# First attention of a two-layer encoder: where the values of the last four heads are projected among the filler work

## The chip, the cores and the metric

The kernel runs on one core of one Trainium2 chip. The metric is device time in microseconds (us) of one execution; lower is better. Engines are named as in the profile: PE (TensorE, matrix products), PEld (its weight loads), DVE (VectorE), ACT (ScalarE), POOL (GpSimd) and SP (SyncE, which here only issues DMAs).

## The reference

A sequence of 512 positions with 1024 features passes two layers. The first is multi-head latent attention with 8 heads and a feed-forward block, the second chunked attention on shared keys and values with a feed-forward block. The change touches only the first attention. Cut to that, it computes:

```python
a = h @ w_a
cq, ckv, kr = split(a, [384, 384 + 256])
q  = (rms_norm(cq, g_q) @ w_uq)          # 8 heads x (128 + 64 rotary)
kv = (rms_norm(ckv, g_kv) @ w_ukv)       # 8 heads x (128 keys + 128 values)
s  = (q_nope . k_nope + q_rope . k_rope) * scale, masked by chunks of 64
o  = softmax(s) @ v
y  = o @ w_o
```

Inputs and output are float32.

## The kernel before, in words

**Numbers as pairs.** A float32 operand of a product is split in a high part (a cast on ACT, L144) and the rest (a subtraction on DVE, L145). A product is then three matmuls (`mm3`, L355 to L358): high by high, low by high, high by low. So each weight chunk and each result that is multiplied again costs one ACT and one DVE instruction. In the profile the weight parts are called `whi` and `wlo`.

**Weights.** `feed` holds a list of weight chunks in the order of their use (L724 to L753). A chunk is loaded by SP into one of five `raw` buffers, split into one of three pairs `whi`, `wlo`, and used. `feed.next` hands out the next chunk and the list must be in the order in which the work asks; `feed.ahead` splits one chunk in advance. The 1024-column chunk `w_uv[1]` holds the value weights of heads 4 to 7, a 640-column chunk `w_qk[h]` the query and key weights of head h, `w_uqr[0]` and `w_uqr[1]` the rotary query weights.

**PSUM.** Results of matmuls go to eight banks (`bank`, L92): four with the tag "mm" for all projections and the products with the values, two "s" for scores, two "t" for transposes. A tile keeps its bank until ACT and DVE have read it.

**First attention.** `attention` (L513) walks through 8 heads x 4 blocks of 128 queries. At each step it computes the scores of a block, transposes the probabilities of an earlier one, and at every fourth step does a head's product with the values (`pv`, L1013). Between these it weaves in units of filler work, so that PE has something to do while softmax runs on DVE and ACT. The filler is the generator `fill_a` (L986): values of heads 0 to 3 (`values_a(0)`, four tiles of 128 positions, 8 units), the norm of the queries, the rotary queries of heads 0 to 3 (`rotary(0)`), the rotary key, head 0's queries and keys (`heads_a(0)`, 6 units), and so on. `start_a(0)` runs the filler up to head 0; `attention` then takes 13 units before the first scores (the argument `first` at L1038), and from there about 1.6 units a step. `until` takes as many units as are needed to reach a mark: head h's mark before its scores, the mark "v" before a product with the values.

**Names.** `values_a(c)` (L888) writes a values tile `b` into `va0` to `va3`; its split is brought forward by 90 places of priority where c is 1 (L899). `heads_a(h)` (L924) makes `qh`, `ql` (high and low part of the queries) and `kh`, `kl` (keys), each a buffer of the 15 of tag "a", which also hold the four rotary query tiles `qr` of a half. `rotary` (L902) makes `ra`, `rb`, `rh`, `rl` and copies parts of them into `qr` by 16 small DMAs. `rotary_key` (L977) makes `kr1` and `kr2`. `query_norm` (L971) makes `nsq`, with one power on POOL (L452). `cqh`, `cql` and `ckh`, `ckl` are the low-rank queries and keys that all these projections read.

The order on each engine is set at build time by a scheduler, by the order of the code and the priorities (`first(n)`); on the chip each engine runs its own list strictly in that order and waits on semaphores for the others.

Of the kernel before, what the change touches and what calls it, by code (L numbers as in the profile page):

```python
# [21 lines left out]
H_A, NOPE, ROPE, VD = 8, 128, 64, 128  # L22
# [46 lines left out]
def trunk(ctx: ExitStack, tc: tile.TileContext, a, out):  # L69
# [16 lines left out]
    def U(dt=F32, name="u"):  # L86
        return up.tile([P, S], dt, tag="u", name=name_(name), bufs=NU)
# [4 lines left out]
    def bank(tag="mm", name="b"):  # L92
        return ps.tile([P, S], F32, tag=tag, name=name_(name), bufs={"mm": 4, "s": 2, "t": 2}[tag])

    def small(name="sm"):
        return sp.tile([P, 4], F32, tag="small", name=name_(name))
# [38 lines left out]
    @contextmanager  # L135
    def first(n):

        tc.cur_priority -= n
        yield
        tc.cur_priority += n  # L140


    def split(dst_hi, dst_lo, src):
        return (nc.scalar.copy(dst_hi, src),  # L144
                V.tensor_tensor(dst_lo, src, dst_hi.bitcast(F32), op=OP.subtract))  # L145
# [203 lines left out]
    feed = Feed()  # L349
# [5 lines left out]
    def mm3(o, l, r, start, stop):  # L355
        nc.tensor.matmul(o, l[0], r[0], start=start, stop=False)  # L356
        nc.tensor.matmul(o, l[0], r[1], start=False, stop=False)  # L357
        nc.tensor.matmul(o, l[1], r[0], start=False, stop=stop)  # L358
# [24 lines left out]
    def cut(t, c):  # L383
        return t[0][:, c], t[1][:, c]
# [80 lines left out]
    def spread(col, first=0):  # L465

        b = bank("t", "bc")
        for i in range(col.shape[1]):
            nc.tensor.transpose(b[:, (first + i) * P:(first + i + 1) * P],
                                col[:, i:i + 1].to_broadcast([P, P]), ident)  # L470
        return b
# [255 lines left out]
        feed.add(a["w_aq"][k], 768)  # L727
    feed.add(a["w_uv"][0], 1024)
    feed.add(a["w_uqr"][0], 768)
    feed.add(a["w_qk"][0], 640)  # L730
    feed.add(a["w_uv"][1], 1024)
    for h in range(1, H_A):
        if h == 4:
            feed.add(a["w_uqr"][1], 768)
        feed.add(a["w_qk"][h], 640)
# [50 lines left out]
    for k in range(KT):  # L786
        h, l = U(F32R, "xh"), U(F32R, "xl")
# [68 lines left out]
    for j in range(2):  # L856
        V.tensor_tensor(ckv[j], ckv[j], rkv, op=OP.mult)
        h, l = U(F32R, "ckh"), U(F32R, "ckl")
# [9 lines left out]
    for j in range(3):  # L868
        h, l = U(F32R, "cqh"), U(F32R, "cql")
# [9 lines left out]
    def A(name):  # L879
        return pool[0].tile([P, S], F32R, tag="a", name=name_(name), bufs=15)  # L880
# [7 lines left out]
    def values_a(c):  # L888

        w = feed.next(1024, False)  # L890
        for tt in range(NQT):
            if tt == 1:
                feed.ahead()
            b = bank()
            ts_ = slice(tt * P, (tt + 1) * P)
            for k in range(2):
                mm3(b, cut(cks[k], ts_), w(k * S, S), k == 0, k == 1)
                yield True
            with first(90 if c else 0):  # L899
                split(va[tt][:, 0, c * S:(c + 1) * S], va[tt][:, 1, c * S:(c + 1) * S], b)  # L900

    def rotary(half):  # L902

        b = [bank() if half else bank("s") for _ in range(2)]
        yield from proj(2, 3, 3, cqs, b, False)
        pc = []
        for (m1, m2, op) in ((cos, sin, OP.subtract), (sin, cos, OP.add)):
            ta, tb = U(name="ra"), U(name="rb")
            V.tensor_tensor(ta, b[0], m1, op=OP.mult)
            V.tensor_tensor(tb, b[1], m2, op=OP.mult)  # L910
            V.tensor_tensor(ta, ta, tb, op=op)
            h, l = U(F32R, "rh"), U(F32R, "rl")
            split(h, l, ta)
            pc.append((h, l))
        for hh in range(4):
            q = A("qr")
            for part in range(2):
                for i in range(2):
                    d = (part * 2 + i) * 32
                    nc.sync.dma_start(q[d:d + 32].bitcast(F32),  # L920
                                      pc[i][part][hh * 32:(hh + 1) * 32].bitcast(F32))
            qr[4 * half + hh] = q

    def heads_a(h):  # L924
        bq = bank()
        w = feed.next(640, False)
        for k in range(3):
            if k == 2:
                feed.ahead()
            mm3(bq, w(k * P, P), cqs[k], k == 0, k == 2)  # L930
            yield True
        qh, ql, kh, kl = (A(n) for n in ("qh", "ql", "kh", "kl"))
        split(qh, ql, bq)
        bk = bank()
        for k in range(2):
            mm3(bk, w((3 + k) * P, P), cks[k], k == 0, k == 1)
            yield True
        split(kh, kl, bk)
        qk_a[h] = qh, ql, kh, kl
        yield h  # L940

    def out_first(rhs):


        late = []
        for i in range(2):
            while i and not fill.scored:
                yield False
            b = [bank("s" if i else "mm") for _ in range(2)]
            firsts.extend(b)  # L950
            for c in range(2):
                w = feed.next(1024, False)
                for k in range(4 * c, 4 * c + 4):
                    if k == 4 * c + 1:
                        feed.ahead()

                    def step(k=k, b=b, w=w):
                        while len(rhs) <= k:
                            yield False
                        for j in range(2):  # L960
                            mm3(b[j], w(k % 4 * 256 + j * P, P), rhs[k], k == 0, k == KT - 1)
                            yield True

                    if k < KT - 1:
                        yield from step()
                    else:
                        late.append(step())
        for t in late:
            yield from t

    def query_norm():  # L971
        for j in range(3):
            sq_.add(b2[j])
        rq = rstd_of_scaled(sq_.total(), QL, r0)
        V.tensor_scalar(nsq, rq, -((NOPE + ROPE) ** -0.5), None, op0=OP.mult)

    def rotary_key():  # L977

        nc.gpsimd.tensor_tensor(sik[:64], kr[64:], sik[64:], op=OP.mult)
        nc.gpsimd.tensor_tensor(kr[:64], kr[:64], cos[:64], op=OP.mult)  # L980
        nc.gpsimd.tensor_tensor(kr[:64], kr[:64], sik[:64], op=OP.add)
        for e in (LO, HI):
            nc.scalar.copy(kr1[e], kr[:64])
            V.tensor_tensor(kr2[e], kr[:64], kr1[:64].bitcast(F32), op=OP.subtract)

    def fill_a():  # L986
        yield from values_a(0)
        query_norm()
        yield from rotary(0)
        rotary_key()  # L990
        yield from heads_a(0)
        yield from values_a(1)
        yield "v"
        for h in range(1, H_A):
            if h == 4:
                yield from rotary(1)
            yield from heads_a(h)
        yield from out_first(osp)

    def start_a(h):  # L1000
        fill.until(h)
        qh, ql, kh, kl = qk_a.pop(h)
        r = qr.pop(h)

        def qk(o, qt, n):
            q_ = slice(qt * P, (qt + 1) * P)
            nc.tensor.matmul(o, qh[:, q_], kh[:, :n], start=True, stop=False)
            nc.tensor.matmul(o, qh[:, q_], kl[:, :n], start=False, stop=False)
            nc.tensor.matmul(o, ql[:, q_], kh[:, :n], start=False, stop=False)
            nc.tensor.matmul(o, r[:, q_], kr1[:, :n], start=False, stop=False)  # L1010
            nc.tensor.matmul(o, r[:, q_], kr2[:, :n], start=False, stop=True)

        def pv(pth, ptl):  # L1013
            fill.until("v")
            o = bank()
            v_ = slice(h * VD, (h + 1) * VD)
            for kt in range(NQT):
                q_ = slice(kt * P, S)
                mm3(o[:, q_], (va[kt][:, 0, v_], va[kt][:, 1, v_]), (pth[:, kt, q_], ptl[:, kt, q_]),
                    kt == 0, kt == NQT - 1)  # L1020
            V.reciprocal(sums, sums)
            of = U(name="of")
            nc.scalar.copy(of, o)

            def rest():
                V.tensor_tensor(of, of, spread(sums), op=OP.mult)
                oh, ol = U(F32R, "oh"), U(F32R, "ol")
                split(oh, ol, of)
                osp.append((oh, ol))

            return rest

        sums = small("sums")
        return Head(qk, lambda n: mask[:, S - n:], lambda qt: nsq[:, qt:qt + 1], pv, sums)

    firsts = []
    fill = Filler(fill_a())
    attention(H_A, start_a, fill, 13, 8 + 5 * 7 + 6 + 14, False)  # L1038
    fill.drain()
# [592 lines left out]
    fill = Filler(fill_b())  # L1632
# [108 lines left out]
```

## Time and profile before

| | |
|---|---|
| median of 3 timed runs | 1124.07 us (1122.27 to 1124.4) |
| profiled execution, own time | 1122.24 us |
| its span, first to last instruction | 1120.5 us |
| instructions | 18982 |
| mean granted clock of PE | 0.998 |

Tables of the profile give the busy time of an engine and its share of the span. A row of the timeline has the start in us from the span's start, the duration, the engine, the line of the kernel, the operation, the tile that is written and those that are read, their shapes, and the number of merged instructions; in brackets stands the idle time before it and what ended that. Instructions on PE overlap, so the step from one start to the next says more than a duration. A row of the waits names who waited for whom, the total in us, how many times, and the longest.

### The profile page before, as it was taken

The numbers are of one execution on the slowest core, as the hardware profiler recorded it, in microseconds if no ns is written. First come the engines' busy times: TensorE is split into PE (matmuls) and PEld (weight loads), VectorE is DVE, ScalarE is ACT, GpSimd is POOL, SyncE is SP. The second block draws the span as 40 slices with busy tenths as digits, with TensorE's granted clock in tenths as the row PEclk, the third lists the DMA queues.
The fourth block names the chain that finished last, engine by engine and source line by source line (L and its number), as shares of the span: only waits on it lengthen the run. The fifth ranks groups of instructions, "written<-read, shape, count | busy, mean of one in ns | idle before, by whom it ended". The sixth has DMA issues, their size and how long they took to land.

```text
span 1120.5 us, 18982 instructions
## 1 busy us (share of the span) xinstructions
PE 1104.6 (99%) x6973; PEld 984.4 (88%) x6973; DVE 932.4 (83%) x1671; ACT 685.5 (61%) x1339; POOL 69.1 (6%) x106
## 2 busy tenths in 40 slices
PE   9999999999999999999999999999999999999997
PEld 6788889999999998887788888889999999998885
DVE  6787737999989889978868887758999899889977
ACT  6476636755555556768435767656755555566675
POOL 1200000000000001400000000000000000002402
PEclk9999999999999999999999999999999999999999
DMA  7342216323232358861556565635423322459923
GB/s 234 107 117 67 85 56 227 133 70 107 94 127 95 125 167 241 145 202 29 193 150 168 142 178 148 165 103 181 148 78 95 125 84 95 142 169 289 172 57 76
DMA packets 62990, 150.85 MB, mean 135 GB/s; under 512 B 8432, under 2 KB 10224, under 8 KB 62896
## 3 DMA queue, kind: packets, MB, share of 16 engines
q1 hardware_dynamic: 55552, 136.61, 38.7%
q0 software_dynamic: 6912, 12.59, 6.8%
q8 instruction: 55, 0.90, 0.3%
q10 hardware_dynamic: 432, 0.44, 0.1%
q14 instruction: 39, 0.32, 0.1%
HBM read 119.52 MB, written 9.63 MB: 115 GB/s over the span
## 4 chain that ended last, share of the span: by engine, by line
PE 46%; DVE 3%; DMA 2%; issue 1%; ACT 1%; POOL 0%; SPq 0%; POOLq 0%; DVEq 0%; ACTq 0%
PE al L1446 8%; PE b L356 6%; PE b L357 6%; PE b L358 6%; PE be L1446 4%; PE al L1197 4%; PE be L1197 3%; PE ga L1446 2%; PE pt L508 1%; PE de L1197 1%; PE ga L1197 1%; PE b L1600 1%; PE b L1599 1%; PE sc L1592 1%; PE sc L1591 1%
## 5 line engine op out<-in xcount | busy, mean ns | idle before, releaser
L144 ACT CAST whi<-raw 128x1024 fp32r<-128x1024 f32 (+3 forms) x224 | 225.5, 1007 | 212.6 <-PE al L1446 73.0
L145 DVE TENSOR_TENSOR wlo<-raw,whi 128x1024 fp32r<-128x1024 f32 (+3 forms) x224 | 261.3, 1168 | 57.7 <-ACT whi L144 54.3
L1446 PE MATMUL al<-th,whi 128*128 128x256 f32 x432 | 123.0, 285 | 0.4 <-DVE ut L1458 0.3
L1446 PE MATMUL al<-th,wlo 128*128 128x256 f32 x432 | 121.2, 281 | 0.0
L1446 PE MATMUL al<-tl,whi 128*128 128x256 f32 x432 | 121.0, 280 | 0.0
L356 PE MATMUL b<-xh,whi 128*128 128x512 f32 (+1 forms) x304 | 117.6, 387 | 0.1
L357 PE MATMUL b<-xl,whi 128*128 128x512 f32 (+1 forms) x304 | 113.0, 372 | 0.1
L358 PE MATMUL b<-xh,wlo 128*128 128x512 f32 (+1 forms) x304 | 112.4, 370 | 0.3 <-DVE wlo L145 0.3
L174 DVE TENSOR_TENSOR raw<-raw,raw 128x1024 f32<-128x1024 f32 x72 | 86.7, 1220 | 1.2 <-DMA raw<-in_w_pair 0.9
L1446 PEld LDWEIGHTS al<-th,whi 128*128 128x128 f32 x432 | 81.3, 188 | 2.9 <-DVE ut L1458 0.8
L1446 PEld LDWEIGHTS al<-th,wlo 128*128 128x128 f32 x432 | 81.3, 188 | 0.4 <-DVE wlo L145 0.4
L1446 PEld LDWEIGHTS al<-tl,whi 128*128 128x128 f32 x432 | 81.3, 188 | 0.0
L496 ACT ACTIVATE p<-p,mn 128x128 f32<-128x128 f32 (+1 forms) x96 | 54.0, 563 | 39.5 <-DVE mn L494 38.4
L145 DVE TENSOR_TENSOR ptl<-pt,pth 128x128 fp32r<-128x128 f32 (+1 forms) x96 | 46.7, 487 | 29.4 <-ACT pth L144 23.7
L358 PEld LDWEIGHTS b<-xh,wlo 128*128 128x128 f32 x304 | 57.5, 189 | 10.1 <-DVE wlo L145 0.7
L144 ACT CAST whi<-wd 128x512 fp32r<-128x512 f32 x86 | 49.9, 620 | 26.8 <-PE al L1197 11.9
L145 DVE TENSOR_TENSOR wlo<-wd,whi 128x512 fp32r<-128x512 f32 x86 | 56.5, 689 | 11.5 <-ACT whi L144 11.2
L356 PEld LDWEIGHTS b<-xh,whi 128*128 128x128 f32 x304 | 57.7, 190 | 7.5 <-ACT xh L148 1.0
L357 PEld LDWEIGHTS b<-xl,whi 128*128 128x128 f32 x304 | 57.7, 190 | 7.3 <-DVE xl L149 1.4
L144 ACT CAST pth<-pt 128x128 fp32r<-128x128 f32 (+1 forms) x96 | 40.4, 421 | 26.6 <-PE pt L508 25.6
L1197 PE MATMUL al<-whi,ph 128*128 128x512 f32 x132 | 51.9, 393 | 0.5 <-ACT y L1258 0.5
L1197 PE MATMUL al<-whi,pl 128*128 128x512 f32 x132 | 51.5, 391 | 0.0
(309 smaller groups left out, 3267.4 us busy)
## 6 DMA issues: line engine op xcount, KB each, us to landing
raw<-in_w_pair SPq DMA_DIRECT2D x72, 512.0 KB, 3.6
wd<-in_w_down SPq DMA_DIRECT2D x54, 256.0 KB, 5.6
raw<-in_w_o SPq DMA_DIRECT2D x16, 512.0 KB, 3.5
raw<-in_w_gu SPq DMA_DIRECT2D x16, 512.0 KB, 3.8
raw<-in_w_down SPq DMA_DIRECT2D x16, 512.0 KB, 4.1
raw<-in_w_qkb SPq DMA_DIRECT2D x16, 512.0 KB, 3.5
wd<-in_w_down POOLq DMA_DIRECT2D x22, 256.0 KB, 5.6
wd<-raw POOLq DMA_DIRECT2D x22, 256.0 KB, 4.2
```

Of the source, the lines that this page charges most:

```text
L144: return (nc.scalar.copy(dst_hi, src), V.tensor_tensor(dst_lo, src, dst_hi.bitcast(F32), op=OP.subtract))
L145: V.tensor_tensor(dst_lo, src, dst_hi.bitcast(F32), op=OP.subtract))
L174: V.tensor_tensor(t, x, y, op=OP.add)
L356: nc.tensor.matmul(o, l[0], r[0], start=start, stop=False)
L357: nc.tensor.matmul(o, l[0], r[1], start=False, stop=False)
L358: nc.tensor.matmul(o, l[1], r[0], start=False, stop=stop)
L496: nc.scalar.activation(p[:, :n], p[:, :n], AF.Exp, bias=mn[:, :1], scale=-1.0, accum_out=self.sums[:, qt:qt + 1])
L508: nc.tensor.transpose(t[:, kt * P:(kt + 1) * P], p[:, kt * P:(kt + 1) * P], ident)
L1197: nc.tensor.matmul(to[e], l[c], r[d], start=j < 4 and k == 0 and n == 0, stop=k == NF // 2 - 1 and n == 2, skip_group_check=True)
L1446: nc.tensor.matmul(o, l[c], r[d], start=first_ and n == 0, stop=k == K2 - 1 and n == 2, skip_group_check=True)
L1591: nc.tensor.matmul(o, q1[:, e, q_], k1[:, e, :n], start=True, stop=False)
L1592: nc.tensor.matmul(o, q1[:, e, q_], k2[:, e, :n], start=False, stop=True)
```

## The change: the second half of the values goes behind head 2

The values of heads 4 to 7 (`values_a(1)`) and their mark "v" move in the filler from behind head 0's queries and keys to behind head 2's; the weight list is reordered to match; and only heads 4 to 7 ask for the mark before their product with the values.

```diff
     feed.add(a["w_uv"][0], 1024)
     feed.add(a["w_uqr"][0], 768)
-    feed.add(a["w_qk"][0], 640)
-    feed.add(a["w_uv"][1], 1024)
-    for h in range(1, H_A):
+    for h in range(H_A):
+        if h == 3:
+            feed.add(a["w_uv"][1], 1024)
         if h == 4:
             feed.add(a["w_uqr"][1], 768)
         feed.add(a["w_qk"][h], 640)
...
         rotary_key()
-        yield from heads_a(0)
-        yield from values_a(1)
-        yield "v"
-        for h in range(1, H_A):
+        for h in range(H_A):
+            if h == 3:
+                yield from values_a(1)
+                yield "v"
             if h == 4:
                 yield from rotary(1)
             yield from heads_a(h)
...
         def pv(pth, ptl):
-            fill.until("v")
+            if h >= 4:
+                fill.until("v")
```

No instruction is added or taken away. What the scheduler makes of it is seen in the engines' lists. Each row has the line, the operation, the tile written and the tiles read, the shape, and in brackets the engines that it waits for.

First PE, in the 13 units ahead of the first scores. Before, behind the second values tile of the second half (`b_166`) the third one (`b_167`) begins:

```order
L356 MATMUL b_166_735<-whi_154_697,ckh_102_465 128x512
L357 MATMUL b_166_735<-wlo_155_698,ckh_102_465 128x512
L358 MATMUL b_166_735<-whi_154_697,ckl_103_466 128x512
L356 MATMUL b_167_744<-whi_154_697,ckh_100_460 128x512 [waits DVE_49]
L357 MATMUL b_167_744<-wlo_155_698,ckh_100_460 128x512
```

Now, at that place, head 1's keys (`b_170`) end, head 0's first score matmul follows (`sc_181`), and head 2's queries (`b_171`) begin:

```order
L357 MATMUL b_170_742<-ckl_103_466,whi_154_697 128x512
L358 MATMUL b_170_742<-ckh_102_465,wlo_155_698 128x512
L1007 MATMUL sc_181_786<-kh_158_706,qh_156_704 128x128 [waits DVE_49,Activation_49]
L356 MATMUL b_171_751<-cqh_111_525,whi_164_729 128x512 [waits DVE_49]
L357 MATMUL b_171_751<-cql_112_526,whi_164_729 128x512
```

The four values tiles stand behind head 2's keys now, in between the scores of head 0; from the end of the fourth on PE's list is as it was.

Second DVE, while PE is there. Before:

```order
L462 TENSOR_TENSOR r2_134_614<-r_133_612,r_81_356 128x4 [waits Pool_49]
L145 TENSOR_TENSOR rl_143_649<-ra_140_643,rh_142_648 128x512 [waits Activation_49]
L975 TENSOR_SCALAR nsq_537<-r2_134_614 128x4 [waits DVE_49]
L145 TENSOR_TENSOR va0_543<-b_162_720,va0_543 128x512 [waits Activation_49]
L909 TENSOR_TENSOR ra_144_652<-b_135_617,sin_91_406 128x512
L910 TENSOR_TENSOR rb_145_653<-b_136_618,cos_92_407 128x512
L145 TENSOR_TENSOR va1_544<-b_166_735,va1_544 128x512 [waits Activation_49]
L911 TENSOR_TENSOR ra_144_652<-ra_144_652,rb_145_653 128x512 [waits DVE_49]
L145 TENSOR_TENSOR va2_545<-b_167_744,va2_545 128x512 [waits Activation_49]
L145 TENSOR_TENSOR rl_147_658<-ra_144_652,rh_146_657 128x512 [waits Activation_49]
L145 TENSOR_TENSOR ql_157_705<-b_152_688,qh_156_704 128x512 [waits Activation_49]
```

Now (`wlo_174` is the low part of the moved value weights, `wlo_186` that of head 3's query and key weights):

```order
L145 TENSOR_TENSOR wlo_174_761<-raw_153_695,whi_173_760 128x1024 [waits PE_49,Activation_49]
L145 TENSOR_TENSOR rl_143_649<-ra_140_643,rh_142_648 128x512 [waits Activation_49]
L909 TENSOR_TENSOR ra_144_652<-b_135_617,sin_91_406 128x512
L910 TENSOR_TENSOR rb_145_653<-b_136_618,cos_92_407 128x512
L145 TENSOR_TENSOR wlo_186_804<-raw_163_727,whi_185_803 128x640 [waits DMAHW6_49,PE_49,Activation_49]
L911 TENSOR_TENSOR ra_144_652<-ra_144_652,rb_145_653 128x512 [waits DVE_49]
L145 TENSOR_TENSOR rl_147_658<-ra_144_652,rh_146_657 128x512 [waits Activation_49]
L984 TENSOR_TENSOR kr2_118_539<-kr_104_469,kr1_117_538 64x512 [waits Activation_49]
L984 TENSOR_TENSOR kr2_118_539<-kr_104_469,kr1_117_538 64x512
L145 TENSOR_TENSOR ql_157_705<-b_152_688,qh_156_704 128x512 [waits Activation_49]
L145 TENSOR_TENSOR kl_159_707<-b_160_710,kh_158_706 128x512 [waits Activation_49]
```

The three `va` rows that emptied values tiles are gone from among the rotary rows, and weight splits of 1024 and 640 columns and the two `kr2` stand ahead of `ql_157`, which empties head 0's query tile `b_152`.

Third ACT, at the same time. Before:

```order
L144 CAST whi_171_771<-raw_153_695 128x640 [waits DVE_49,DMAHW3_49,PE_49,Activation_49]
L144 CAST rh_142_648<-ra_140_643 128x512 [waits DVE_49]
L144 CAST va0_543<-b_162_720 128x512 [waits PE_49]
L144 CAST va1_544<-b_166_735 128x512 [waits PE_49]
L144 CAST va2_545<-b_167_744 128x512 [waits PE_49]
L144 CAST rh_146_657<-ra_144_652 128x512 [waits DVE_49]
L144 CAST qh_156_704<-b_152_688 128x512
```

Now:

```order
L144 CAST whi_173_760<-raw_153_695 128x1024 [waits DVE_49,DMAHW3_49,PE_49,Activation_49]
L144 CAST rh_142_648<-ra_140_643 128x512 [waits DVE_49]
L144 CAST whi_185_803<-raw_163_727 128x640 [waits DMAHW6_49,PE_49,Activation_49]
L144 CAST rh_146_657<-ra_144_652 128x512 [waits DVE_49]
L983 CAST kr1_117_538<-kr_104_469 64x512 [waits Pool_49]
L983 CAST kr1_117_538<-kr_104_469 64x512
L144 CAST qh_156_704<-b_152_688 128x512
```

The casts of the values tiles are gone from here, and a weight cast and the two halves of the rotary key stand ahead of `qh_156`.

## The prediction

> **What bounds the kernel now.** I read the page's busy times first, then stretches of the window in which the change lies, then the waits of TensorE (PE) there, then the instructions themselves.
>
> ```profile
> PE 1104.6 (99%) x6973; PEld 984.4 (88%) x6973; DVE 932.4 (83%) x1671; ACT 685.5 (61%) x1339; POOL 69.1 (6%) x106
> ```
>
> PE is busy for 99% of the span, so time that PE loses is lost for good unless a later wait of PE shrinks by as much. By the two orders of instructions, PE's rows 230 to 306 are rearranged and every other row of PE is the same; VectorE (DVE) differs in its rows 77 to 124 and ScalarE (ACT) in 55 to 86. In the trace of before PE's rows 230 to 306 run from 56.68 to 73.37 us.
>
> ```profile
> 56.70:60.00 3.30, 3.18 (x14) 2.35 (x13) 2.73 (x8) 2.24 (x4) 1.02 (x1) 1.00 0.47 130
> 60.00:63.40 3.40, 3.27 (x14) 2.36 (x13) 3.38 (x7) 2.11 (x5) 0.00 (x0) 1.00 0.46 107
> 63.40:66.80 3.40, 3.40 (x17) 2.80 (x16) 3.31 (x7) 3.37 (x7) 0.00 (x0) 1.00 0.41 96
> ```
>
> The columns are the stretch, its length, then busy us of PE, PEld, DVE, ACT and POOL, and the granted clock. PE hardly idles here, and DVE is as full as PE from 60 to 66.8. So nothing is to be gained on PE but 0.12 + 0.13 us and what the overlap hides; and DVE has no room for being asked earlier. Where PE does wait:
>
> ```profile
> 56.68 0.39 PE L356 MATMUL b<-whi,ckh 128*128 128x512 f32 x1
> 59.17 0.39 PE L358 MATMUL b<-whi,ckl 128*128 128x512 f32 x1
> 59.69 0.50 PE L356 MATMUL b<-whi,ckh 128*128 128x512 f32 x1
> 60.95 0.40 PE L358 MATMUL b<-whi,ckl 128*128 128x512 f32 x1
> 61.48 0.50 PE L356 MATMUL b<-whi,ckh 128*128 128x512 f32 x1
> PEld b L356 <- DVE va L145: 1.1, 2, 0.6
> ```
>
> Between the first two rows lie eleven steps of 0.227 us (2.49 / 11), the pace of 512-column matmuls. Behind 59.17 and behind 60.95 a step takes 0.52 and 0.53, each time at the first matmul of a values tile. The third and fourth values tile wait until DVE's `va` has emptied the PSUM bank of the first and second: four banks serve all projections (tag "mm"), and the two others hold head 0's queries and keys, which ACT and DVE have not got to. That is the key to the change: **banks, emptied by two engines in a fixed order**.
>
> **The change, step by step.** In the new order, head 1's queries and keys stand where two and a half values tiles stood. Each head's tiles keep their banks until `ql` and `kl` are written; a values tile is emptied early, by its raised priority. So at head 2's first matmul (PE row 246) the four banks hold head 0's q and k and head 1's q and k, and none is emptied. Which comes free first, and when? DVE's row 96 (`ql` of head 0). I follow DVE there from lengths of before.
>
> ```profile
> 52.92 1.22 DVE L145 TENSOR_TENSOR wlo<-raw,whi 128x1024 fp32r<-128x1024 f32 x1
> 55.32 0.82 DVE L145 TENSOR_TENSOR wlo<-raw,whi 128x640 fp32r<-128x640 f32 x1
> 56.73 0.17 DVE L448 TENSOR_SCALAR v<-v 128x4 f32<-128x4 f32 x1
> 56.97 1.02 POOL L452 TENSOR_TENSOR r<-v,mhalf 128x4 f32<-128x4 f32 x1 [9.16 <-DVE v L448]
> 56.70 0.73 ACT L144 CAST whi<-raw 128x640 fp32r<-128x640 f32 x1 [3.16 <-PE b L357]
> 49.87 1.08 ACT L144 CAST whi<-raw 128x1024 fp32r<-128x1024 f32 x1
> ```
>
> DVE's row 77 now splits 640 weight columns in place of 1024, 0.40 less, so `v` comes at 56.33, POOL's power ends at about 57.6 and `r`, `nsq` are written by 57.9. The 1024-column split has moved into row 87. Its ACT half can't start before 56.70, when PE has read the buffer it goes into, and ends at 57.78. So DVE starts row 87 at 57.9.
>
> ```profile
> 59.55 0.68 DVE L909 TENSOR_TENSOR ra<-b,sin 128x512 f32<-128x512 f32 x1
> 60.15 0.68 DVE L910 TENSOR_TENSOR rb<-b,cos 128x512 f32<-128x512 f32 x1
> 62.06 0.62 ACT L144 CAST rh<-ra 128x512 fp32r<-128x512 f32 x1
> 63.65 1.26 ACT L983 CAST kr<-kr 64x512 fp32r<-64x512 f32 x2
> 64.52 1.38 DVE L984 TENSOR_TENSOR kr<-kr,kr 64x512 fp32r<-64x512 f32 x2
> ```
>
> Starts on DVE are 0.60 apart for 512 columns, 0.74 for 640 and 1.13 for 1024. Row 87: 57.92 to 59.05. `rl`, `ra`, `rb`: to 60.85. `wlo` of head 3's weights, which stands ahead now: to 61.59 (its ACT half waits for PE's last read of head 1's weights, near 60.0, and is done by 60.8). `ra`: ends at 62.27. ACT's `rh` then takes 62.31 to 62.93, DVE's `rl` 62.96 to 63.56, the two `kr2` 1.38, to 64.94; ACT has written `qh` by 64.7. So `ql` runs from 64.94 to **65.6**, and head 2's matmul starts at 65.7. PE gets there after 15 matmuls of 0.227 from 56.68 and one short score matmul, at 60.1.
>
> **Term 1: a new wait of 5.5 us.** Its ends: 5.0 (ten steps read to 0.05 each) and 6.6 (POOL's power has a row twice as long):
>
> ```profile
> 28.52 2.07 POOL L452 TENSOR_TENSOR r<-v,mhalf 128x4 f32<-128x4 f32 x1 [13.98 <-DVE v L448]
> ```
>
> Behind the waiting matmul stands all of PE, the scores of head 0 too, and with them DVE's and ACT's softmax. Nothing covers it: PE runs in order, and the values matmuls (24 of 0.227, 5.4 us) that filled just this time are behind it now.
>
> **Term 2: minus 0.6.** The two waits of before (0.52 and 0.53 less 0.23 each) go, as values tiles meet banks that DVE empties at 66.2 (`kl`), 66.8 and 67.4, before PE asks.
>
> **Term 3: plus 0.4.** The emptying of four values tiles and of head 2's keys now falls among head 0's softmax. Head 2's `kl` takes the first buffer of the 15 that carry these operands, and waits for head 0's last score; behind it on DVE wait `va`, head 0's last mask step and the exponent on ACT, and at the end the last `ptl`, which the first product with the values reads.
>
> ```profile
> 71.76 0.40 PE L356 MATMUL b<-ckh,whi 128*128 128x512 f32 x1
> 72.61 0.74 DVE L494 CUSTOM_DVE_ANT_0 p<-sc,mask,nsq 128x512 f32<-128x512 f32 x1
> 74.01 0.72 ACT L496 ACTIVATE p<-p,mn 128x512 f32<-128x512 f32 x1
> 76.80 0.69 DVE L145 TENSOR_TENSOR ptl<-pt,pth 128x512 fp32r<-128x512 f32 x1
> 78.48 0.39 PE L357 MATMUL b<-ptl,va 128*128 128x512 f32 x1
> ```
>
> PE's stream asks for `ptl` 6.72 after head 0's scores (78.48 - 71.76); before, it was there at 77.49, 1.0 early. Now: 0.3 for the last score, 0.60 `kl`, 0.60 `va`, 0.67 mask, 1.0 exponent with its sum, then ACT's values copy, weight split, two exponents and three `pth`, and DVE's last 640 columns and `ptl`: about 7.1, so 0.4 late (0 to 0.8).
>
> **Term 4: the clock.** The trace has one long pause of PE, its end, and one long cold stretch, its start.
>
> ```profile
> 1112.65:1116.07 3.42, 0.47 (x3) 0.05 (x1) 2.51 (x6) 0.72 (x2) 1.00 (x1) 1.00 0.21 77
> 1116.07:1119.48 3.41, 0.00 (x0) 0.00 (x0) 1.39 (x3) 0.00 (x0) 0.00 (x0) 0.50 0.64 231
> 1.19 4.02 PE L113 MATMUL warm<-idle 128*128 128x512 bf16 x9 [1.19 <-DVE idle L110]
> 6.10 0.78 PE L357 MATMUL b<-xl,whi 128*128 128x512 f32 x1
> 6.69 0.42 PE L358 MATMUL b<-xh,wlo 128*128 128x512 f32 x1
> 6.95 0.40 PE L356 MATMUL b<-xh,whi 128*128 128x512 f32 x1
> ```
>
> After 0.47 us of work in the 3.42 us up to 1116.07 the clock falls to 0.50, 2.95 us after the last work ended (1112.65 + 0.47). At the start a 512-column matmul takes 0.45 (4.02 over nine), twice the 0.23 of later, and the short step returns at 6.7, 5.5 us after PE's first work. The new pause has one 128-column matmul in 5.5 us, near its end, when `kh` is there (65.1), and behind the last one's end (60.25) 4.8 us of nothing. That is longer than 2.95, so the clock likely falls. Then PE runs at half speed for between 3.0 us (as short as the fall took) and 5.5 (as at the start), and half of that is lost: 1.5 to 2.8. Without a fall the price is nothing. I take 1.75, nearer to the short end, as the start's 5.5 had waits for its operands in it.
>
> The Trainium skill, "TensorE: Matmul & The Clock Gate", section "What's actually happening", says that PE falls to half its clock after an idle window of about 3.4 us and comes back after a busy one, and that the windows run freely, whatever the kernel does. By that page one window at half speed would cost an estimated 1.7 us, and a pause of 5.5 us can also end with no whole idle window in it. The trace agrees on the fall: 0.47 us of work in 3.42 was little enough.
>
> **What costs nothing.** The values' weights are asked for one place later in SP's queue:
>
> ```profile
> 37.95 0.35 SPq L287 DMA_DIRECT2D raw<-in_w_qk  x1
> raw<-in_w_uv SPq DMA_DIRECT2D x2, 512.0 KB, 5.0
> qr<-rl SPq DMA_DIRECT2D x16, 64.0 KB, 2.0
> ```
>
> The issue near 38 now carries 512 KB, landing at 43; ACT reads it at 56.7. The 16 small rotary copies keep their count and shift by under 1 us; head 0's last is issued near 64 and there by 66.5, while PE reads it at about 69.8. If these covers went, each would add its delay to the same wait.
>
> **Sum.** 5.5 - 0.6 + 0.4 + 1.75 = 7.05 us. The profiled execution took 1122.24 us (span 1120.5 and 1.74 around it), so 1129.3 on its scale. The three timed runs have a median of 1124.07, 1.8 above it, which would give 1131.1. I predict between them, **1130.2 us**.
>
> **Rivals.**
> - *The clock stays up.* For it: the pause is only about 2 us longer than the time the clock took to fall, and a matmul stands in it. Against: no shorter pause is shown that kept it. Time: 1122.24 + 5.3 = 1127.5 (1129.4 by the median).
> - *The bank is free in time* (the other side). The wait for `ql` decides: if DVE wrote head 0's `ql` by 60.1, no pause would come, and only the two old waits would go, 1122.24 - 0.6 = 1121.6, no change. For it: head 0's queries are complete at 55.3, and only order keeps `ql` back. Against: DVE has 7.0 us of work and waits in line from 57.9 on, ACT's `rh` among it. The time is level with `ql` at 60.7, and 0.2% longer with `ql` at 63.
> - *The delay is taken up later.* PE's waits after 80 us, ten kinds, come to 5.3 us:
>
> ```profile
> PE b L357 <- DVE wlo L149: 1.3, 1, 1.3
> ...
> PE b L356 <- DVE ra L909: 0.2, 1, 0.2
> ```
>
>  If all of them were for work that doesn't follow PE, 7.05 - 5.3 = 1.75 would be left: 1124.0. Against: each is for DVE, ACT or POOL working on what PE made just before, and so shifts with PE.
>
> **How the numbers follow.** Forecast with the clock's fall 0.80; clock stays 0.14; taken up later 0.03; bank in time 0.03. The range runs from the second case's low end (1122.24 + 5.0 - 0.6 + 0 = 1126.6, drawn in to 1127.0) to the forecast's high end by the median (1124.07 + 6.6 - 0.6 + 0.8 + 2.8 = 1133.7): 1127.0 to 1133.5. Slower by over 0.2% (2.2 us, about what a measurement of this kernel can tell from no change) is 0.94, within it 0.05, faster 0.01.
>
> **What would show it.** In the profile after: PE idle of about 5.5 us from 60.1 to 65.7, ended by DVE's `ql`, L145; a stretch of granted clock 0.50 behind it and steps of 0.45 there; no wait of PE at the values tiles; a short wait for `ptl` at head 0's first product with the values; from there on the same stream as before, about 7 us later. I am wrong if PE waits for under 3 us there, if `ql` is written long before 65, or if the shift at 80 us isn't that at the end.

## The result, and the profile after

| | before | after |
|---|---|---|
| median, 4 timed runs each | 1123.17 us (1120.22 to 1124.4) | 1128.85 us (1128.65 to 1130.33) |
| ratio | | 1.0064 [1.0051, 1.0078] |
| profiled execution, own time | 1122.24 us | 1130.33 us |
| mean granted clock of PE | 0.998 | 0.995 |

The kernel became slower. The ratio 1.0064 means 0.64% of 1123.17 = 7.2 us (5.7 to 8.8 by the interval). It isn't the quotient of the two medians of four, which lie 5.7 us apart, at the low end of the interval. On another chip (e5 below) the medians lie 7.4 us apart. The figure predicted was 1130.2, in a range from 1127.0 to 1133.5.

The page's line of busy times, after:

```profile
PE 1107.8 (98%) x6973; PEld 987.2 (87%) x6973; DVE 933.2 (83%) x1671; ACT 685.3 (61%) x1339; POOL 69.0 (6%) x106
```

PE has as many instructions as before and is busy 3.2 us longer (1107.8 against 1104.6): the same work ran slower somewhere. The rest of the loss must be idle time. The two longest waits of PE after, then the waits of its weight loads (PEld) between 54 and 90 us:

```profile
PE sc L1007 <- ACT kh L144: 5.0, 1, 5.0
PE b L357 <- DVE wlo L149: 1.3, 1, 1.3
...
PEld sc L1007 <- ACT kh L144: 5.4, 1, 5.4
PEld b L356 <- DVE ql L145: 0.2, 1, 0.2
```

The wait of 1.3 was there before; the one of 5.0 is new, and the two at values tiles (1.1 together) are gone. The profile puts the new pause down to head 0's first score, which lacks `kh`. The very next matmul, head 2's first, then lacks a bank until DVE's `ql`, but only 0.2 of its wait is left to show. When two matmuls in a row have to wait, the first one's wait covers most of the second's, so the instruction behind a long wait is worth a look as well. PE's timeline has them one behind the other.

```profile
56.74 0.39 PE L356 MATMUL b<-cqh,whi 128*128 128x512 f32 x1
59.92 0.39 PE L358 MATMUL b<-ckh,wlo 128*128 128x512 f32 x1
65.30 0.47 PE L1007 MATMUL sc<-kh,qh 128*128 128x128 f32 x1 [4.99 <-ACT kh L144]
65.79 0.79 PE L356 MATMUL b<-cqh,whi 128*128 128x512 f32 x1
66.81 0.63 PE L358 MATMUL b<-cqh,wlo 128*128 128x512 f32 x1
67.23 0.63 PE L356 MATMUL b<-cqh,whi 128*128 128x512 f32 x1
71.45 0.40 PE L356 MATMUL b<-whi,ckh 128*128 128x512 f32 x1
```

The first row is PE's first rearranged one, at 56.74 (56.68 before); the second is the last of head 1's 15 matmuls. At their pace the next would start at 59.92 + 0.23 = 60.15. One score matmul of 0.06 between them makes 60.21 for head 2's first, which starts at 65.79: 5.6 us. The step from 66.81 to 67.23 is 0.42 where it was 0.23. Head 2's 15 matmuls take 71.45 - 65.79 = 5.66 us in place of 15 x 0.227 = 3.41: another 2.25.

DVE's timeline shows what the bank waited for, and one row of ACT what the score waited for:

```profile
57.98 1.23 DVE L145 TENSOR_TENSOR wlo<-raw,whi 128x1024 fp32r<-128x1024 f32 x1
61.66 0.69 DVE L911 TENSOR_TENSOR ra<-ra,rb 128x512 f32<-128x512 f32 x1
63.03 0.69 DVE L145 TENSOR_TENSOR rl<-ra,rh 128x512 fp32r<-128x512 f32 x1 [0.68 <-ACT rh L144]
63.64 1.38 DVE L984 TENSOR_TENSOR kr<-kr,kr 64x512 fp32r<-64x512 f32 x2
65.04 0.69 DVE L145 TENSOR_TENSOR ql<-b,qh 128x512 fp32r<-128x512 f32 x1
64.65 0.59 ACT L144 CAST kh<-b 128x512 fp32r<-128x512 f32 x1
```

DVE works without a gap from 57.98, waits once for ACT's `rh`, and ends `ql` at 65.04 + 0.69 = 65.73; PE goes on at 65.79. ACT is hardly earlier: it writes `qh`, which `ql` reads, from 64.17 to 64.76 and `kh` from 64.65 to 65.24. So head 0's tiles stand late in the lists of both engines. Stretches of after, with the columns as before (length, busy us of PE, PEld, DVE, ACT, POOL, then the granted clock), cut where the clock changes:

```profile
60.12:63.54 3.42, 0.18 (x1) 0.00 (x0) 2.74 (x5) 1.86 (x3) 0.00 (x0) 1.00 0.41 96
63.54:66.95 3.41, 1.63 (x4) 1.25 (x5) 3.37 (x7) 2.67 (x5) 0.00 (x0) 0.50 0.37 87
66.95:70.36 3.41, 3.41 (x10) 2.64 (x9) 0.58 (x1) 0.33 (x1) 0.00 (x0) 0.50 0.46 106
70.36:73.77 3.41, 3.41 (x19) 2.84 (x18) 1.92 (x4) 2.55 (x4) 0.00 (x0) 1.00 0.59 192
```

The clock is at half from 63.54 to 70.36, 6.82 us, with PE at work on the projections in the last 4.57 of them. Half of 4.57 is 2.3, which is the 2.25 just read from the matmuls.

So the loss has two parts in one place, a pause and the cold stretch behind it. The experiments ask whether the banks are its cause, what holds `ql` back, and whether the clock's share is real.

### The profile page after: what moved, and what is told of

Same layout as the page of the kernel before. It is cut to its first block, busy times and chain, and to the rows that moved or that the text cites. A ratio compares the mean times of both kernels' runs of the same rounds, so it can differ in the third digit from the quotient of the medians.

```text
span 1128.5 us, 18984 instructions
## 1 busy us (share of the span) xinstructions
PE 1107.8 (98%) x6973; PEld 987.2 (87%) x6973; DVE 933.2 (83%) x1671; ACT 685.3 (61%) x1339; POOL 69.0 (6%) x106
## 4 chain that ended last, share of the span: by engine, by line
PE 45%; DVE 4%; DMA 2%; issue 1%; ACT 1%; POOL 0%; SPq 0%; POOLq 0%; DVEq 0%; ACTq 0%
PE al L1447 8%; PE b L356 5%; PE b L357 5%; PE b L358 5%; PE be L1447 4%; PE al L1198 4%; PE be L1198 3%; PE ga L1447 2%; PE de L1198 1%; PE ga L1198 1%; PE pt L508 1%; PE b L1601 1%; PE b L1600 1%; PE sc L1593 1%; DVE wlo L145 1%
```

## The experiments

The first four ran on one chip, where before took 1121.2 us (median of 20 runs, 1119.72 to 1123.95), the last four on another, where it took 1120.03 (21 runs, 1118.83 to 1121.67). Ratios are against these.

### e1_own_buffers: the rotary tiles get buffers of their own

The theory says that head 0's `ql` is late because it stands late in DVE's list (and `qh` in ACT's), and that it stands there because `qh`, `ql`, `kh`, `kl` share 15 buffers with the four rotary query tiles `qr`, handed out in the order of the code. Here the same 15 buffers are divided, 4 and 11.

```diff
-        return pool[0].tile([P, S], F32R, tag="a", name=name_(name), bufs=15)
+        if name == "qr":
+            return pool[0].tile([P, S], F32R, tag="qr", name=name_(name), bufs=4)
+        return pool[0].tile([P, S], F32R, tag="a", name=name_(name), bufs=11)
```

> The changed kernel, with the four rotary query tiles in buffers of their own (4) and the heads' operands in the 11 others, so that head 0's ql need not be ordered behind the rotary copies; in DVE's list ql of head 0 moves from row 96 to row 85. Bank theory (PE pauses because head 0's q and k hold their PSUM banks until DVE and ACT reach them behind the rotary work): ql is written before 59 us, no wait of PE over 1 us between 56 and 75 us, granted clock 1.00 throughout, ratio to before 0.998 to 1.002. Rival (the scores of head 0 wait for the rotary work itself, and the banks are only what the wait looks like): PE still idles 4 to 5 us somewhere before 68 us, ratio 1.004 to 1.007.

Measured: 1120.73 us, ratio 0.9994 [0.9984, 1.0005]. The loss is gone. DVE's row, PE's only wait between 54 and 90 us, and two stretches:

```profile
55.55 0.68 DVE L145 TENSOR_TENSOR ql<-b,qh 128x512 fp32r<-128x512 f32 x1
...
PE sc L1009 <- DVE mn L494: 0.3, 1, 0.3
...
60.00:63.40 3.40, 3.40 (x18) 2.81 (x16) 3.40 (x7) 3.03 (x6) 0.00 (x0) 1.00 0.47 109
63.40:66.80 3.40, 3.40 (x22) 2.98 (x21) 3.35 (x6) 2.49 (x5) 0.00 (x0) 1.00 0.37 87
```

`ql` now starts 9.5 us earlier (55.55 against 65.04; of that 0.9 is this execution's earlier start, with head 1's first matmul at 55.83 against 56.74), and ACT's `qh` moves by as much, from 64.17 to 54.67. PE is busy for all of 60 to 66.8, and the clock stays at 1.00. The values are still behind head 2. So the place of the values costs nothing by itself; **the order in which the banks come free is the cause, and the shared buffers set that order**. How the scheduler gets from shared buffers to such an order is read from the code; no run shows it. One thing moved with it: head 0's first score now stands behind head 2's matmuls, so this run removes the wait for `kh` along with that for the bank. Which of the two would hold PE without the other is the question of e4.

### e2_dummies: PE kept at work in the pause

Twenty more matmuls, whose result nobody reads, stand behind head 1's keys, 20 x 0.227 = 4.5 us in the pause of after. They add work that the reference doesn't have. If the clock's share is real, it goes while the wait stays.

```diff
+            if h == 2:
+                o = bank("t", "dummy")
+                for _ in range(20):
+                    nc.tensor.matmul(o, cks[0][0][:, :P], cks[0][0], start=True, stop=True)
```

> The changed kernel with 20 matmuls of 512 columns added behind head 1's keys, whose result nobody reads: they fill 4.5 of the 5.4 us in which PE idles and change no wait. Clock theory (2.1 us of the loss are matmuls at half clock behind the pause): the first matmul of head 2 stands at 65.8 us as in the changed kernel, the steps behind it are 0.23 and not 0.43, the granted clock is 1.00 from 60 to 75 us, and the kernel is 2.1 us shorter than the changed one: ratio to before 1.004 to 1.005. Rival (the clock costs nothing, since DVE and ACT set the pace there): same time as the changed kernel, ratio 1.0064.

Measured: 1126.75 us, ratio 1.0048 [1.0033, 1.0063], granted clock 0.998 to 0.999 in every run. PE's timeline and two stretches:

```profile
59.22 4.70 PE L995 MATMUL dummy<-ckh 128*128 128x512 f32 x20
64.39 0.33 PE L1011 MATMUL sc<-kh,qh 128*128 128x128 f32 x1 [0.47 <-ACT kh L144]
64.88 0.50 PE L356 MATMUL b<-cqh,whi 128*128 128x512 f32 x1 [0.17 <-DVE ql L145]
65.67 0.40 PE L356 MATMUL b<-cqh,whi 128*128 128x512 f32 x1
...
63.40:66.80 3.40, 2.76 (x12) 1.89 (x11) 3.17 (x5) 1.91 (x4) 0.00 (x0) 1.00 0.45 106
66.80:70.20 3.40, 3.40 (x18) 2.89 (x17) 1.59 (x3) 2.34 (x4) 0.00 (x0) 1.00 0.46 102
```

Head 2 still has to wait for the bank: it starts 9.1 us behind head 1's first matmul (64.88, against 59.22 less 15 x 0.227), as in after (65.79 - 56.74). But the clock stays at 1.00 and the steps are short at once. There is more work on PE and, by the ratios, a shorter time than that of after (1.0048 against 1.0064), but the two intervals overlap. This pair was run once more to size the difference (e5, e6).

### e3_behind_head1: the values one head earlier

The values stand behind head 1 in place of head 2, in the list of weights and in the filler.

```diff
-        if h == 3:
+        if h == 2:
             feed.add(a["w_uv"][1], 1024)
...
-            if h == 3:
+            if h == 2:
                 yield from values_a(1)
```

> The values stand behind head 1's queries and keys, one head earlier than in the change. Bank theory: the four banks are full after head 1 all the same, so the first values tile waits for head 0's ql until 65 to 66 us, PE idles 5 us, the clock falls: ratio 1.005 to 1.007. Rival (each head that is put ahead of the values costs its share): half of the loss, ratio 1.003.

Measured: 1125.88 us, ratio 1.0039 [1.0024, 1.0054]. PE's timeline and the clock's first two stretches:

```profile
57.87 0.39 PE L356 MATMUL b<-ckh,whi 128*128 128x512 f32 x1
62.37 0.47 PE L1007 MATMUL sc<-kh,qh 128*128 128x128 f32 x1 [3.66 <-ACT kh L144]
62.87 0.80 PE L356 MATMUL b<-whi,ckh 128*128 128x512 f32 x1
...
57.34:60.75 3.41, 1.37 (x7) 0.79 (x5) 3.38 (x8) 2.00 (x4) 0.00 (x0) 1.00 0.41 96
60.75:64.16 3.41, 1.77 (x4) 1.40 (x5) 3.36 (x7) 2.54 (x5) 0.00 (x0) 0.50 0.40 94
```

The time alone can't tell the two readings apart: 1.0039 is below the 1.005 to 1.007 that I had expected, and its interval holds the rival's 1.003. The trace can. The mechanism is there, one head earlier: it is now a values tile that finds four full banks. Head 1's last three matmuls start at 57.87, so PE could go on at about 58.6; it does at 62.87, 4.3 us later. I had expected a pause of 5 us. DVE's rows of this run show why it is shorter:

```profile
53.38 1.22 DVE L145 TENSOR_TENSOR wlo<-raw,whi 128x1024 fp32r<-128x1024 f32 x1
55.92 0.82 DVE L145 TENSOR_TENSOR wlo<-raw,whi 128x640 fp32r<-128x640 f32 x1 [0.57 <-ACT whi L144]
62.12 0.69 DVE L145 TENSOR_TENSOR ql<-b,qh 128x512 fp32r<-128x512 f32 x1
```

The 1024-column split of the values' weights stands ahead of POOL's power here, and a 640-column split fills the time of the power. In after DVE idles for 1.1 us there (from 56.58, when `v` is written, to 57.70) and splits the 1024 columns behind it. `ql` starts 2.9 us earlier than in after (62.12 against 65.04); 1.6 of that is this execution's earlier start (head 1's first matmul at 55.15 against 56.74), so 1.3 is gained, as much as the pause is shorter (4.3 against 5.6). **The pause was mis-sized because a weight split changed its place in DVE's list**, which I had not followed.

### e4_spare_banks: head 2 writes into the two other banks

Head 2's queries and keys take the two banks of tag "t", which are free at that time. Then they need not wait for head 0's `ql`, and the score's `kh` is what is left.

```diff
-        bq = bank()
+        bq = bank("t" if h == 2 else "mm")
...
-        bk = bank()
+        bk = bank("t" if h == 2 else "mm")
```

> The changed kernel, with head 2's queries and keys in the two transpose banks, which are empty at that time. Bank theory: head 2's 15 matmuls run on without a wait to 63.5 us, then PE waits for kh and for a bank for the first values tile until 66 to 66.7 us: 2.5 to 3.1 us idle in place of 5.4; such a pause is about as short as the 2.95 us that the clock took to fall at the end of the kernel, so it may stay at 1.00: 2 to 2.5 us over before, ratio 1.0018 to 1.0025 (1.004 if the clock falls). Rival (PE is held by something else than the banks): ratio 1.006.

Measured: 1125.49 us, ratio 1.0034 [1.0024, 1.0044]. PE's timeline and three stretches:

```profile
61.89 0.39 PE L356 MATMUL b<-ckh,whi 128*128 128x512 f32 x1
65.07 0.33 PE L1007 MATMUL sc<-kh,qh 128*128 128x128 f32 x1 [2.34 <-ACT kh L144]
65.69 0.79 PE L356 MATMUL b<-whi,ckh 128*128 128x512 f32 x1 [0.30 <-DVE ql L145]
...
61.97:65.38 3.41, 1.07 (x5) 0.48 (x3) 3.27 (x5) 3.36 (x7) 0.00 (x0) 1.00 0.35 83
65.38:68.79 3.41, 3.11 (x10) 2.67 (x10) 3.01 (x7) 3.14 (x6) 0.00 (x0) 0.50 0.45 105
68.79:72.21 3.42, 3.42 (x12) 2.88 (x11) 0.35 (x1) 0.81 (x3) 0.00 (x0) 0.50 0.81 250
```

Head 2's 15 matmuls ran through to 61.89 + 3 x 0.227 = 62.57 with no wait, and then PE stood until 65.69: 3.1 us, within the 2.5 to 3.1 that I had expected. The pause is shorter by what head 2 put into it, and the bank of the next tile is again the one that `ql` frees. The score's `kh`, at 65.07, comes 0.6 before that. So either wait alone would hold PE nearly as long; both operands come from the same late place.

The clock is the miss: it was to stay up, and fell, although PE had worked for 1.07 of the 3.41 us before and its longest gap was 2.34 us. The granted clock of the ten runs lies between 0.995 and 0.998, so in some of them it may not have fallen, or for less; only one has a trace. The time points the same way: 0.34% of 1121.2 is 3.8 us (2.7 to 4.9), while the traced execution lost 3.1 in the pause and ran at half speed from 65.69 to 72.21, which is worth up to 3.3 more.

### e5_change_again and e6_dummies_again: the clock's share once more

The changed kernel and e2's kernel, both as they were, side by side on the second chip.

> The changed kernel once more, on the chip and in the rounds of the three below, so that they can be set against it directly. Both theories: 1.005 to 1.008 of before, granted clock 0.995 to 0.996.

> The kernel with the 20 added matmuls in PE's pause once more. Clock theory: 2 us under the changed kernel of the same rounds, ratio to before 1.0035 to 1.0055, clock 0.998 or 0.999 in every run. Rival (the clock costs nothing): the same as the changed kernel within 0.5 us.

| | median | ratio | granted clock |
|---|---|---|---|
| e5_change_again | 1127.44 us (5 runs) | 1.0065 [1.0052, 1.0078] | 0.995 to 0.996 |
| e6_dummies_again | 1125.93 us (5 runs) | 1.0048 [1.0034, 1.0062] | 0.998 to 0.999 |

Both repeat. By the ratios the added matmuls save 0.0065 - 0.0048 = 0.0017, or 1.9 us of 1120, by the medians 1.5. The intervals overlap, and e6's slowest run, 1128.21 us, is slower than four of e5's five, so these times alone don't prove it. The traces do. From PE's first rearranged matmul to head 1's first score every kernel has the same 77 matmuls (97 with the twenty added), and the time between these two starts is free of what the rest of the kernel does:

| | first rearranged matmul | head 1's first score | between | against before |
|---|---|---|---|---|
| before | 56.68 | 73.37 | 16.69 us | |
| after | 56.74 | 80.41 | 23.67 us | +6.98 |
| e5, the same kernel | 55.61 | 79.46 | 23.85 us | +7.16 |
| e2, twenty more | 55.82 | 77.36 | 21.54 us | +4.85 |
| e6, twenty more | 56.65 | 78.19 | 21.54 us | +4.85 |
| e1, own buffers | 55.83 | 72.29 | 16.46 us | -0.23 |
| e3, behind head 1 | 55.15 | 77.55 | 22.40 us | +5.71 |
| e4, spare banks | 55.77 | 77.74 | 21.97 us | +5.28 |
| e7, before with own buffers, first | 55.39 | 71.48 | 16.09 us | -0.60 |
| e8, own buffers, first | 54.88 | 72.13 | 17.25 us | +0.56 |

The clock's share is what the twenty matmuls save: 2.1 to 2.3 us (23.67 and 23.85 less 21.54). In the trace of e5 the score waits as long as in after (4.99 us):

```profile
64.16 0.47 PE L1007 MATMUL sc<-kh,qh 128*128 128x128 f32 x1 [4.99 <-ACT kh L144]
64.66 0.79 PE L356 MATMUL b<-cqh,whi 128*128 128x512 f32 x1
66.10 0.63 PE L356 MATMUL b<-cqh,whi 128*128 128x512 f32 x1
```

### e7 and e8: can either kernel gain from the divided buffers?

Head 0's two splits are also brought forward by 90 places of priority, in e7 on the kernel before, in e8 on e1's kernel. e7 also has e1's division of the buffers.

```diff
-        split(qh, ql, bq)
+        with first(90 if h == 0 else 0):
+            split(qh, ql, bq)
...
-        split(kh, kl, bk)
+        with first(90 if h == 0 else 0):
+            split(kh, kl, bk)
```

> The kernel before, with the rotary query tiles in 4 buffers of their own, the heads' operands in 11, and head 0's splits brought forward by 90. Bank theory: the two waits of 0.3 us at the third and fourth values tile of before are all there is to gain, as their banks come free earlier: 0 to 0.6 us less, ratio 0.999 to 1.000. Rival (head 0's early scores bring the whole attention forward): 2 us or more less, ratio 0.998 or lower.

> The changed kernel with buffers of their own for the rotary tiles, and head 0's splits brought forward by 90 as well. Bank theory: no pause is left to shorten, so the same as with the buffers alone, ratio to before 0.998 to 1.0005. Rival (head 0's early scores bring the attention forward): ratio 0.998 or lower.

Measured: e7 1119.45 us, ratio 0.9995 [0.9986, 1.0004]; e8 1120.51 us, ratio 1.0006 [0.9997, 1.0015]. In e7 PE has no wait left between 54 and 90 us; in e8 one:

```profile
PE sc L1011 <- DVE mn L494: 0.9, 1, 0.9
```

By their times neither can be told from before. The two waits of before were worth 0.6 us, which is 0.05%: e7's ratio has that size, and its interval is wider than that; the table above shows these 0.60 us in its trace. No kernel here beats before by more than a measurement of the whole time shows.

One of e8's eleven runs had a mean granted clock of 0.948 and took 1120.19 us, no more than the others. It has no trace, so what happened there stays open; it shows that a low mean clock by itself doesn't say that time was lost.

## Why the prediction was right, point by point

- **Bound.** Right: PE, in order, with nothing over the pause. e1 gives it all back.
- **Which tile frees the first bank.** Right: head 0's `ql`. Predicted to run from 64.94 to 65.6; it ran from 65.04 to 65.73. The walk along DVE's list held because each duration came from the trace of before. Row 87 was put at 57.92 and started at 57.98.
- **Term 1, plus 5.5.** Measured 5.6. What the prediction gave as "ended by DVE's `ql`" the profile names `kh`; e4 shows that the two waits are nearly equal, with `ql`'s the longer by 0.6 (0.5 in after: 65.73 against 65.24).
- **Term 2, minus 0.6.** Right: no values tile waits in after.
- **Term 3, plus 0.4.** Wrong; it was nothing. The step that failed: "Head 2's `kl` takes the first buffer of the 15 that carry these operands, and waits for head 0's last score". `kl` waited for L1008, three matmuls ahead of the last score. L1008 reads head 0's `qh` and `kl`, so the buffer was one of theirs, and not, as the sum took it, one that is read up to the last score. The rows of after, of PE and DVE:

```profile
77.87 0.39 PE L1008 MATMUL sc<-kl,qh 128*128 128x512 f32 x1
78.57 0.40 PE L1011 MATMUL sc<-kr,qr 128*128 128x512 f32 x1
78.30 0.69 DVE L145 TENSOR_TENSOR kl<-b,kh 128x512 fp32r<-128x512 f32 x1 [0.44 <-PE sc L1008]
79.51 0.74 DVE L494 CUSTOM_DVE_ANT_0 p<-sc,mask,nsq 128x512 f32<-128x512 f32 x1
84.21 0.68 DVE L145 TENSOR_TENSOR ptl<-pt,pth 128x512 fp32r<-128x512 f32 x1
85.52 0.39 PE L357 MATMUL b<-ptl,va 128*128 128x512 f32 x1
```

`kl` starts at 78.30, when L1008 is through and L1011 has not begun. The mask step follows at 79.51, and `ptl` ends at 84.89, 0.6 before PE asks for it at 85.52. Counted from the matmul behind the scores (78.81), as the prediction counts, `ptl` was done after 6.1 us in place of 7.1; `kl` began 0.5 before that matmul in place of 0.3 behind it, which is 0.8 of the difference.

- **Term 4, plus 1.75 for the clock.** Right that it falls; the size was 2.25. The prediction let half speed last between 3.0 and 5.5 us of PE's work and took a value near the short end; it was 4.57, inside that range. The half clock lasted 6.82 in all, but its first 2.25 us lay in the pause (63.54 to 65.79), where it costs next to nothing. The comparison behind the forecast (a pause of 4.8 us against the 2.95 that one fall had taken) isn't a rule: behind PE's last work the fall came after 3.2 us in after and after 2.0 in e3. Here the pause was long enough for either.
- **Sum.** 5.6 - 0.6 + 0 + 2.25 = 7.25, against 7.05 predicted: the errors of terms 3 and 4 nearly cancel, which is luck. Between the two matmuls of the table above the change costs 6.98 us in after's trace and 7.16 in e5's; the 0.1 to 0.3 short of 7.25 isn't accounted for. The timed difference is 7.2 by the ratio. Head 1's first score stands 7.04 later than before. At the last matmul of the two profiled executions the shift is 8.07:

```profile
1120.80 0.39 PE L1198 MATMUL be<-whi,pl 128*128 128x512 f32 x1
```

Before, that matmul (there L1197) started at 1112.73. The further 1.0 us comes in later stages. The prediction had named such a difference as a sign of being wrong. It need not come from the change: from head 1's first score to the last matmul it is 1040.39 us in after and 1037.45 in e5, which is the same kernel, and 1039.36 in before, between the two.

- **The time.** 1130.2 was put between the profiled execution of before and the median of three runs, 1124.07. The median of four is 1123.17; with 7.05 on it the forecast would have been 1130.2 as well. The median measured is 1.4 below that, as the medians lie only 5.7 apart.
- **The rivals.** "The clock stays up" would have given 1127.5; e2 shows that it can be had with PE at work in the pause, at a ratio of 1.0048 (1127.5 is 1.0047 of 1122.24). "The bank is free in time" was given 1121.6; e1 is that case, and its result is no difference, as the prediction had it. "The delay is taken up later" didn't come: at the last matmul PE's stream is no less late than at 80 us.

## What to carry to other kernels

Work that looks like mere filler can also be what lets another engine empty the banks: before moving it, list which tiles hold each bank at the first matmul behind, and walk the emptying engine's list to the instruction that frees the first of them. If that instruction stands late though its operand is long there, look for a buffer shared with a later-finished tile; here dividing 15 buffers into 4 and 11 made the change free. For a pause of PE count the pause and, if the clock falls, the slow stretch behind it, here 2.25 us on top of 5.6. In these traces the clock fell where PE had a gap of 2.3 us (e4) or more, and stayed up through one of 1.7 (e8, before 765.87); between the two none was seen.

## What the runs showed of the hardware that had not been expected

The clock fell after stretches in which PE was far from idle: 1.07 us of work in 3.41 (e4) and 1.37 in 3.41 (e3), besides 0.18 in 3.42 (after). In e3 it fell 2.0 us after PE's last work had ended (60.75, against 58.32 + 0.39). It stayed up behind these two stretches, the first of e2 and the second of e8, which have the same length and lie whole multiples of it from the clock's changes in their traces (in e2 it fell only behind the next stretch, which was idle):

```profile
1114.48:1117.90 3.42, 1.70 (x8) 1.08 (x6) 2.34 (x5) 0.72 (x2) 0.57 (x1) 1.00 0.30 92
764.00:767.41 3.41, 1.75 (x15) 1.55 (x15) 2.78 (x5) 1.91 (x4) 0.00 (x0) 1.00 0.41 144
```

"TensorE: Matmul & The Clock Gate" of the Trainium skill, section "What's actually happening", speaks of an idle window; by these traces a window with 40% of work (e3) was idle enough, and one with 50% (e2) was not.

In the four traces of after, e3, e4 and e5 the half clock lasted 6.82 or 6.83 us, twice 3.41, whenever PE's work came back within it. The first of its two stretches had 1.63, 1.77, 3.11 and 2.08 us of work, and even e4's 3.11 of 3.41 didn't end it; the next, busy throughout, did. At the start of the same execution of e4 less was enough:

```profile
1.19 3.46 PE L113 MATMUL warm<-idle 128*128 128x512 bf16 x9 [1.19 <-DVE idle L110]
```

These nine matmuls took 4.02 us in before, all at half speed. The 0.56 us saved here are some three matmuls at full speed, so the clock rose after about 2.8 us of work, an estimate. The same section of the Trainium skill has the windows run freely and the clock return after a busy one. The free windows agree with these traces; how busy such a window must be they leave open. Even a short pause can be dear: in e4 work came back 0.3 us behind the fall (65.38 to 65.69) and ran at half speed for the 6.5 us that were left.
